# Late u, k and q tiles of the in projection by a wide and a narrow pass; low parts of every third half by an adding transfer

## The chip, the cores and the metric

The kernel runs on one core of one Trainium2 chip. The metric is the device time of one execution in microseconds (us), as a median of several runs; less is better. TensorE multiplies, VectorE and ScalarE compute on tiles, GpSimd and SyncE here only issue transfers.

## The reference

One decoder block on x of 256 x 2048 in float32. One input projection feeds two groups; their outputs are joined, projected, added to x and normalised; a gated FFN with a short convolution follows.

```python
# in projection: x (256 x 2048) @ w_in, columns split into
#   u 1024 | q 1024 | k 256 | v 256 | q_idx 1024 | k_idx 64 | w_idx 16
# group A: S5 state-space channels on u (64 groups, 64 states), gelu, GLU
# group B: for each query the index scores q_idx . k_idx (relu, weighted by w_idx)
#          choose the 64 best keys; attention of q on k, v over these, with ALiBi
# x = layer_norm(alpha * x + concat(A, B) @ w_out)
# x = layer_norm(alpha * x + conv_ffn(x))          # d_ff = 5632
def _conv_ffn(x, w_up, w_gate, conv_w, conv_b, w_down):
    h = x @ w_up
    hp = jnp.pad(h, ((0, 0), (CONV_WIDTH - 1, 0), (0, 0)))
    hc = conv_b + sum(conv_w[i] * hp[:, i:i + seq] for i in range(CONV_WIDTH))
    return (jax.nn.gelu(hc, approximate=False) * (x @ w_gate)) @ w_down
```

## The kernel before

**Precision.** Every float32 operand of a large product is held as two parts that TensorE reads: a high part, which a ScalarE copy rounds, and a low part, what is left, which VectorE subtracts. A product is three matmuls into one accumulator: `mm3` (L184 to L188) multiplies high by high (L186), low weights by high x (L187), and high weights by low x (L188). In the in projection each has 128 x 128 weights and 256 columns, the 256 positions.

**Weights.** They stream from HBM in halves of 128 x 1024 float32, 512 KB; the two halves of kw have 640 columns. `load` (L119) issues a half's transfer on SyncE's queue into one of three buffers named raw. `fetch` (L127) makes its parts: ScalarE copies raw into wh (L133), VectorE subtracts into wl (L136). wh and wl have four buffers each. `next_half` (L143) keeps four halves ready ahead of the one in use, and what `fetch` records has high priority. `BY_DMA` (L35) is a set of half numbers; it is empty, so the branch at L137 to L140 is not taken.

**Numbers of the halves.** 0 to 7 the first four u tiles (first halves, then second halves), 8 to 15 the late u tiles 4 to 7, 16 to 31 the eight tiles of qi (the index queries), 32 and 33 kw (index keys and weights), 34 to 37 the two k tiles, 38 to 41 v, 42 to 57 the eight q tiles; then GLU, out projection and FFN.

**Tiles.** `ws_tile` (L288) computes one tile of 128 output columns by 256 positions: 16 k tiles of `mm3` from two halves, 48 matmuls, into an accumulator named acc of which there are two. After each k tile `pump` advances the background jobs by a step: `ssm` (the state-space group: its bu matmuls, VectorE work of 128 x 1024 in `ssm_in`, cbd and dd matmuls in `ssm_out`, tables of sines and gelu on ScalarE) and `indexer` (index scores). One ScalarE copy then takes the tile out of PSUM: into qi, kv or q (L303), or into u (L315), where positions are written in even and odd halves. u is moved on by 64 small transfers for the state-space group. v takes x as the weights and both accumulators at once (L683 to L691).

**The FFN's form.** Up and gate tiles use `wide_half` (L194 to L205): x's high and low part lie side by side, so one matmul of 512 columns multiplies high weights by both, and one of 256 columns multiplies low weights by high x. Eight and eight make a half, 32 matmuls a tile. The two results lie in two parts of the accumulator; a ScalarE copy (L1046) and a VectorE add (L1047) join them.

**What sets the order.** A scheduler orders each engine's instructions by its own estimates and the priorities that the code gives; each engine then works in order. ScalarE's sines and gelus stand in a fixed sequence (`in_turn`), since they load different tables.

Of the kernel before, what the change touches and what calls it, by code (L numbers as in the profile page):

```python
# [11 lines left out]
F32R = mybir.dt.float32r  # L12
I32 = mybir.dt.int32
AF = mybir.ActivationFunctionType
ALU = mybir.AluOpType
# [3 lines left out]
P = 128  # L19
S = 256  # L20
# [11 lines left out]
LEAD = 5  # L32
LAG = 5
PACE = 4
BY_DMA = range(0)  # L35


PRM = {}
# [44 lines left out]
def block_kernel(ctx: ExitStack, tc: tile.TileContext, x_t, x_n, prm_d, cst_d, ssm_d, w_in_d, w_kw_d, w_v_d,  # L83
                 w_glu_d, w_out_d, w_up_d, w_gate4_d, w_gate_d, w_down_d, ln_d, out_d):
    nc = tc.nc
    V, A, G, T = nc.vector, nc.scalar, nc.gpsimd, nc.tensor

    def pool(name, bufs=1, **kw):
        return tc.tile_pool(name=name, bufs=bufs, **kw)
# [5 lines left out]
    ahl = ctx.enter_context(pool("ahl"))  # L95
# [23 lines left out]
    def load():  # L119
# [3 lines left out]
        n = state["next"]  # L123
        raws.append((raw, src.shape[1], special.get(n), src if n in BY_DMA else None))
        state["next"] += 1
# [17 lines left out]
    def next_half():  # L143
        while len(ready) < state["ahead"] and state["next"] < len(halves):
            fetch()
        return ready.pop(0)
# [41 lines left out]
        return T.matmul(out, lhsT=lh[0], rhs=rh[1], start=False, stop=stop).ins  # L188

    def act_tiles(what):  # L190
        return [(t[:, :, 0, :], t[:, :, 1, :])
                for t in (ahl.tile([P, 4, 2, S], F32R, name=f"{what}{j}", tag=f"hl{j}") for j in range(4))]

    def wide_half(out, half, tiles, kh):  # L194


        def passes(low):
            for k in range(8):
                r = tiles[(kh * 8 + k) // 4][:, k % 4]
                yield low, half[low][:, k * P:(k + 1) * P], r[:, 0] if low else r  # L200

        steps = list(passes(1)) + list(passes(0)) if kh else list(passes(0)) + list(passes(1))
        for i, (low, w, r) in enumerate(steps):
            ins = T.matmul(out[:, 0] if low else out, lhsT=w, rhs=r, start=kh == 0 and i == 0, stop=kh == 1 and i == 15)  # L204
        return ins.ins  # L205

    def kt_of(tiles, kt):
        h, l = tiles[kt // 4]
        return h[:, kt % 4, :], l[:, kt % 4, :]
# [6 lines left out]
    tmp = ExitStack()  # L216
    at = ctx.enter_context(pool("att", side="right"))
    st = tmp.enter_context(pool("ssmt", side="right"))
    xt = act_tiles("x")
    raw_b = st.tile([P, 2, 512], F32, name="raw_b", tag="t3")  # L220
    raw_c = proj.tile([P, 2, 512], F32, name="raw_c", tag="kv")

# [49 lines left out]
    def acc_tile():  # L272
        return ps.tile([P, 512], F32, name="acc", bufs=2)
# [14 lines left out]
    def ws_tile(evac, m=P):  # L288

        acc = acc_tile()  # L290
        for kt in range(16):
            if kt % 8 == 0:
                half = next_half()
            c = (kt % 8) * m
            mm3(acc[:m, :S], (half[0][:, c:c + m], half[1][:, c:c + m]), kt_of(xt, kt), kt == 0, kt == 15)
            pump()
        with tc.high_priority():
            evac(acc)

    def proj_tile(name, t=None):  # L300
        if t is None:
            t = proj.tile([P, S], F32, name=name)
        ws_tile(lambda acc: A.activation(t, acc[:, :S], AF.Copy))  # L303
        return t

    def proj_four(name):
        t = proj.tile([P, 4, S], F32, name=name)
        return [proj_tile(name, t[:, i]) for i in range(4)]


    ut, yt, hs = [], [], {}

    def u_tile(ct, acc):
        t = proj.tile([P, 2, P], F32, name=f"u{ct}")
        A.activation(t.rearrange("p two k -> p k two"), acc[:, :S].rearrange("p (k two) -> p k two", two=2), AF.Copy)  # L315
        ut.append(t)

    bu = psb.tile([P, 2, 2, 512], F32, name="bu")
# [1 line left out]
    for kh in range(2):  # L320
        for ct in range(4):
            half = next_half()
# [91 lines left out]
    two, p = exp_parts(pc("ldt"))  # L414
# [19 lines left out]
    two, p = exp_parts(tt(dt, a_re, ALU.mult))  # L434
# [59 lines left out]
    for ct in range(8):  # L494
        tp = misc_tile()
        for h in range(2):
            for ri in range(2):
                k = (h * 2 + ri) * P
# [119 lines left out]
    for ct in range(4, 8):  # L618
        if ct == SSM_FROM:
            add_bg(ssm_job, 1)  # L620
        ws_tile(lambda acc: u_tile(ct, acc))


    qit = proj_four("qi0") + proj_four("qi1")
    kw = proj.tile([P, S], F32, name="kw")[0:80]
    ws_tile(lambda acc: A.activation(kw, acc[:80, :S], AF.Copy), m=80)
    ki2 = proj.tile([P, S], F32, name="ki2")
# [52 lines left out]
    for kt in range(16):  # L680
        if kt % 4 == 0:
            half = next_half()
# [75 lines left out]
    mix = [None, None, (post.tile([P, 4, S], F32R, name="mixh"), post.tile([P, 4, S], F32R, name="mixl")), None]  # L758
# [9 lines left out]
    drain()  # L768


    hl_tiles = [ahl.tile([P, 4, 2, S], F32R, name=f"mix{j}", tag=f"hl{j}") for j in range(4)]
    hl = [(t[:, :, 0, :], t[:, :, 1, :]) for t in hl_tiles]
    mix = [hl[0], hl[1], mix[2], hl[3]]
    def glu_products(acc, half, kts):
        for kt in kts:
# [11 lines left out]
    for nt in range(8):  # L787
        h, l = mix[nt // 4]
        if nt < 2:
            acc = first_glu[nt][0]  # L790
        else:
            acc = glu_acc(nt)
# [127 lines left out]
    def row_banks(i):  # L920
# [6 lines left out]
    beside = {2: a01.scores, 3: a01.weights, 6: a00.turn, 7: a10.turn, 9: a00.values, 10: a10.values,  # L927
              11: a11.scores, 12: a11.weights, 14: a01.turn, 17: a01.values, 22: a11.turn, 25: a11.values}
    unit = 0
    with tc.manual_schedule(engines={mybir.EngineType.PE}):  # L930
        for some in (range(4), range(4, 6), range(6, 8)):
# [6 lines left out]
            for db in range(3):  # L938
                for i in some:
                    half = next_half()  # L940
# [97 lines left out]
    with pool("pd", space=PSUM) as pd:  # L1038
        for f in range(NF):
            pu = []  # L1040
            for which in range(1 if f < 4 else 2):
                p = pd.tile([P, 2, S], F32, name=f"pd{which}", bufs=2)
                for kh in range(2):
                    last = wide_half(p, next_half(), h1t, kh)
                t = ff.tile([P, S], F32, name=f"sum{which}", bufs=2)
                A.activation(t, p[:, 1], AF.Copy)  # L1046
                V.tensor_tensor(t, t, p[:, 0], op=ALU.add)  # L1047
                pu.append(t)
            if f < 4:

                if f % 2 == 0:
                    gt = pe0.tile([P, 2, S], F32, name="gt", tag=f"e0{f // 2}")
                with tc.issue_after(last):
                  for b in range(2):
                    T.transpose(gt[:, f % 2, b * 128:(b + 1) * 128], gate4[b][:, f * 128:(f + 1) * 128], ident)
            up, gate = pu if f >= 4 else (pu[0], gt[:, f % 2])
            hc = ff.tile([P, S], F32, name="hc", bufs=2)
            A.activation(hc, up, AF.Identity, scale=pc("cw2", f), bias=pc("cb", f))
            V.scalar_tensor_tensor(hc[:, 1:], up[:, :S - 1], pc("cw1", f), hc[:, 1:], op0=ALU.mult, op1=ALU.add)
            V.scalar_tensor_tensor(hc[:, 2:], up[:, :S - 2], pc("cw0", f), hc[:, 2:], op0=ALU.mult, op1=ALU.add)  # L1060
            in_turn(hc, hc, AF.Gelu)
            done = V.tensor_tensor(act[:, f, :], hc, gate, op=ALU.mult).ins
            if f == 4:
                load_ln(0)
            if f == 16:
                load_ln(1)
            if 8 <= f < 14:

                b, db = (f - 8) // 3, (f - 8) % 3 + 1
                cs = slice(db * 512, (db + 1) * 512)  # L1070
                zs = z[:, b, cs]
                with tc.issue_after(done):
                    V.tensor_tensor(zs, zs, ln_t["g"][:, cs], op=ALU.mult)
                    V.tensor_tensor(zs, zs, ln_t["b"][:, cs], op=ALU.add)
# [107 lines left out]
    for f in range(NF):  # L1182
        if f == NF - 8 * LAG:
            state["ahead"] = 2 * LAG
        hl = act_split(f)
        for d2 in range(2):
            half = next_half()
# [103 lines left out]
```

## Time and profile before

| | us |
|---|---|
| median of three runs | 1108.07 |
| the three runs | 1108.05, 1111.54, 1108.07 |
| the profiled execution | 1109.74 |
| its span in the trace | 1108.0 |
| TensorE busy | 1092.8 (99%) |
| VectorE busy | 740.2 (67%) |
| ScalarE busy | 579.2 (52%) |
| GpSimd busy | 0.2 |

The span is from the first to the last instruction of the trace; the execution's own time has 1.7 us more around it. PE is TensorE, DVE VectorE, ACT ScalarE, POOL GpSimd, SP SyncE. Busy times of matmuls overlap, since each begins before the one ahead of it has ended; the pace is read from their starts. L133 is line 133 of the kernel.

### The profile page before, as it was taken

How to read it: one execution, taken by the hardware profiler on the slowest of the kernel's cores; microseconds unless marked ns; L12 is line 12 of the kernel's file. 1: busy time of each engine (PE TensorE's matmuls, PEld its weight loads, DVE VectorE, ACT ScalarE, POOL GpSimd, SP SyncE). 2: the span in 40 equal slices, each digit the busy share in tenths (PEclk: the TensorE clock that was granted, in tenths of full speed). 3: DMA queues.
4: the chain of work that ended last, by engine and by line, in shares of the span. 5: the costliest groups of instructions: out<-in, count | busy, mean ns of one | idle time of the engine just before them, and what ended most of it. 6: DMA issues, size and time to landing. Idle time of an engine off the chain costs nothing.

```text
span 1108.0 us, 16918 instructions
## 1 busy us (share of the span) xinstructions
PE 1092.8 (99%) x6599; PEld 948.2 (86%) x6599; DVE 740.2 (67%) x1054; ACT 579.2 (52%) x878; POOL 0.2 (0%) x4
## 2 busy tenths in 40 slices
PE   8999999999999999999999999999999999999997
PEld 7899998899778888888888888888888888888885
DVE  6969889687558666677666656565656556565547
ACT  5965664457544765555454545454545445454430
POOL 0000000000000000000000000000000000000000
PEclk9999999999999999999999999999999999999999
DMA  7644434246466455555665555555555566665522
GB/s 254 231 147 136 129 132 170 97 140 241 159 225 206 164 198 191 190 189 190 253 204 190 190 191 189 189 192 190 187 190 189 186 227 220 211 225 198 198 101 76
DMA packets 59311, 204.44 MB, mean 185 GB/s; under 512 B 7264, under 2 KB 10080, under 8 KB 58592
## 3 DMA queue, kind: packets, MB, share of 16 engines
q1 hardware_dynamic: 59232, 203.38, 54.0%
q8 instruction: 51, 0.84, 0.3%
q14 instruction: 28, 0.23, 0.1%
HBM read 200.20 MB, written 2.10 MB: 183 GB/s over the span
## 4 chain that ended last, share of the span: by engine, by line
PE 86%; DVE 7%; ACT 2%; DMA 2%; issue 2%; SPq 1%; ACTq 0%; DVEq 0%
PE pd L204 42%; PE e L188 7%; PE e L187 7%; PE e L186 7%; PE acc L187 3%; PE acc L188 3%; PE acc L186 3%; PE o L186 3%; PE o L188 3%; PE o L187 3%; DVE wl L136 2%; PE misc L650 1%; DMA raw<-in_w_in_dram 1%; ACT wh L133 1%; PE glu L187 1%
## 5 line engine op out<-in xcount | busy, mean ns | idle before, releaser
L136 DVE TENSOR_TENSOR wl<-raw,wh 128x1024 fp32r<-128x1024 f32 x299 | 364.8, 1222 | 251.4 <-ACT wh L133 248.2
L133 ACT ACTIVATE wh<-raw 128x1024 fp32r<-128x1024 f32 x299 | 315.3, 1056 | 251.8 <-PE pd L204 135.7
L204 PE MATMUL pd<-mix,wh 128*128 128x512 f32 x1344 | 321.4, 391 | 0.7 <-ACT gate L1018 0.7
L204 PEld LDWEIGHTS pd<-mix,wh 128*128 128x128 f32 x1344 | 246.7, 188 | 48.8 <-ACT gate L1018 1.1
L204 PEld LDWEIGHTS pd<-mix,wl 128*128 128x128 f32 x1344 | 172.4, 191 | 6.6
L204 PE MATMUL pd<-mix,wl 128*128 128x256 f32 x1344 | 174.8, 283 | 0.0
L186 PE MATMUL acc<-x,wh 128*128 128x256 f32 (+1 forms) x400 | 114.5, 288 | 3.7 <-ACT wh L133 1.8
L187 PE MATMUL acc<-x,wl 128*128 128x256 f32 (+1 forms) x400 | 115.2, 288 | 0.5 <-DVE wl L182 0.3
L188 PE MATMUL acc<-x,wh 128*128 128x256 f32 (+1 forms) x400 | 114.8, 288 | 0.8 <-DVE x L182 0.8
L136 DVE TENSOR_TENSOR wxl<-raw,wxh 128x1024 fp32r<-128x1024 f32 x42 | 51.5, 1225 | 45.8 <-ACT wxh L133 44.1
L186 PEld LDWEIGHTS acc<-x,wh 128*128 128x128 f32 (+1 forms) x400 | 76.3, 191 | 5.8 <-ACT wh L133 2.0
L188 PEld LDWEIGHTS acc<-x,wh 128*128 128x128 f32 (+1 forms) x400 | 76.6, 191 | 3.2 <-issue 1.6
L187 PEld LDWEIGHTS acc<-x,wl 128*128 128x128 f32 (+1 forms) x400 | 76.5, 191 | 3.1 <-issue 1.2
L133 ACT ACTIVATE wxh<-raw 128x1024 fp32r<-128x1024 f32 x42 | 44.6, 1061 | 57.8 <-DMA raw<-in_w_down_dram 25.8
L187 PE MATMUL e<-wh,acthl 128*128 128x512 f32 (+1 forms) x154 | 59.5, 386 | 0.0
L186 PE MATMUL e<-wh,acthl 128*128 128x512 f32 (+1 forms) x154 | 59.4, 387 | 0.0
L188 PE MATMUL e<-wl,acthl 128*128 128x512 f32 (+1 forms) x154 | 58.7, 386 | 0.0
L175 ACT ACTIVATE hc<-hc 128x256 f32<-128x256 f32 x44 | 18.4, 417 | 76.2 <-DVE hc L1060 76.2
L186 PE MATMUL e<-wxh,acthl 128*128 128x512 f32 (+1 forms) x130 | 50.1, 386 | 0.0
L187 PE MATMUL e<-wxh,acthl 128*128 128x512 f32 (+1 forms) x130 | 50.1, 386 | 0.0
L188 PE MATMUL e<-wxl,acthl 128*128 128x512 f32 (+1 forms) x130 | 50.1, 386 | 0.0
L1047 DVE TENSOR_TENSOR sum<-sum,pd 128x256 f32<-128x256 f32 x84 | 34.7, 413 | 0.0
(299 smaller groups left out, 1455.5 us busy)
## 6 DMA issues: line engine op xcount, KB each, us to landing
raw<-in_w_gate_dram SPq DMA_DIRECT2D x88, 512.0 KB, 4.0
raw<-in_w_up_dram SPq DMA_DIRECT2D x88, 512.0 KB, 3.9
raw<-in_w_down_dram SPq DMA_DIRECT2D x88, 512.0 KB, 4.5
raw<-in_w_in_dram SPq DMA_DIRECT2D x51, 512.0 KB, 4.3
raw<-in_w_out_dram SPq DMA_DIRECT2D x32, 512.0 KB, 4.0
raw<-in_w_glu_dram SPq DMA_DIRECT2D x8, 512.0 KB, 3.6
raw<-in_w_v_dram SPq DMA_DIRECT2D x4, 512.0 KB, 3.8
z<-in_x_n_dram SPq DMA_DIRECT2D x1, 2048.0 KB, 10.5
```

The costliest lines, as they stand in the source:

```text
L133: A.activation(h[:, :w], raw[:, :w], AF.Copy)
L136: V.tensor_sub(l[:, :w], raw[:, :w], h[:, :w].bitcast(F32))
L175: ins = A.activation(*args, **kw)
L186: T.matmul(out, lhsT=lh[0], rhs=rh[0], start=start, stop=False)
L187: T.matmul(out, lhsT=lh[1], rhs=rh[0], start=False, stop=False)
L188: return T.matmul(out, lhsT=lh[0], rhs=rh[1], start=False, stop=stop).ins
L204: ins = T.matmul(out[:, 0] if low else out, lhsT=w, rhs=r, start=kh == 0 and i == 0, stop=kh == 1 and i == 15)
L650: T.matmul(banks[e][:, (hp % 2) * w:(hp % 2 + 1) * w], lhsT=qit[hp][r, b * 128:(b + 1) * 128], rhs=ki2[r, 0:w], start=True, stop=True)
L1047: V.tensor_tensor(t, t, p[:, 0], op=ALU.add)
```

## The change

Late u (tiles 4 to 7), the two k tiles and the eight q tiles, 14 tiles, are computed by `wide_tile`: two calls of `wide_half`, with `pump` after each of the 16 narrow matmuls. In a tile's first half the eight wide matmuls come first, in its second half the eight narrow ones. The first four u tiles, qi, kw and v keep `mm3`. A wide tile's two results are joined by `add_parts`, a ScalarE copy and a VectorE add; the FFN uses the same function for the same work as before. u's tiles are now read from PSUM in even and odd halves and written in one piece.

`BY_DMA` holds 13 halves: 20, 23, 26, 29 (qi), 32 (kw), 35 (second half of the first k tile), 38, 41 (v), 44, 47, 50, 53, 56 (q). In these the branch in `fetch` is taken: ScalarE writes raw, negated and rounded like the high part, into wl (L139), and a transfer on GpSimd's queue reads the half from HBM a second time and adds it to wl there (L140), which leaves the low part. VectorE's subtract (L136) is left out for them.

```diff
@@ -32,7 +32,7 @@
 LEAD = 5
 LAG = 5
 PACE = 4
-BY_DMA = range(0)
+BY_DMA = range(20, 58, 3)
 
 
 PRM = {}
@@ -188,10 +188,12 @@
         return T.matmul(out, lhsT=lh[0], rhs=rh[1], start=False, stop=stop).ins
 
     def act_tiles(what):
-        return [(t[:, :, 0, :], t[:, :, 1, :])
-                for t in (ahl.tile([P, 4, 2, S], F32R, name=f"{what}{j}", tag=f"hl{j}") for j in range(4))]
-
-    def wide_half(out, half, tiles, kh):
+        return [ahl.tile([P, 4, 2, S], F32R, name=f"{what}{j}", tag=f"hl{j}") for j in range(4)]
+
+    def both_parts(tiles):
+        return [(t[:, :, 0, :], t[:, :, 1, :]) for t in tiles]
+
+    def wide_half(out, half, tiles, kh, beside=lambda: None):
 
 
         def passes(low):
@@ -202,7 +204,13 @@
         steps = list(passes(1)) + list(passes(0)) if kh else list(passes(0)) + list(passes(1))
         for i, (low, w, r) in enumerate(steps):
             ins = T.matmul(out[:, 0] if low else out, lhsT=w, rhs=r, start=kh == 0 and i == 0, stop=kh == 1 and i == 15)
+            if low:
+                beside()
         return ins.ins
+
+    def add_parts(t, hi, lo):
+        A.activation(t, lo, AF.Copy)
+        V.tensor_tensor(t, t, hi, op=ALU.add)
 
     def kt_of(tiles, kt):
         h, l = tiles[kt // 4]
@@ -216,7 +224,8 @@
     tmp = ExitStack()
     at = ctx.enter_context(pool("att", side="right"))
     st = tmp.enter_context(pool("ssmt", side="right"))
-    xt = act_tiles("x")
+    x_tiles = act_tiles("x")
+    xt = both_parts(x_tiles)
     raw_b = st.tile([P, 2, 512], F32, name="raw_b", tag="t3")
     raw_c = proj.tile([P, 2, 512], F32, name="raw_c", tag="kv")
 
@@ -297,22 +306,37 @@
         with tc.high_priority():
             evac(acc)
 
-    def proj_tile(name, t=None):
+    def wide_tile(evac):
+
+        acc = acc_tile().rearrange("p (two s) -> p two s", two=2)
+        for kh in range(2):
+            wide_half(acc, next_half(), x_tiles, kh, pump)
+        with tc.high_priority():
+            evac(acc[:, 0], acc[:, 1])
+
+    def proj_tile(name, t=None, wide=True):
         if t is None:
             t = proj.tile([P, S], F32, name=name)
-        ws_tile(lambda acc: A.activation(t, acc[:, :S], AF.Copy))
+        if wide:
+            wide_tile(lambda hi, lo: add_parts(t, hi, lo))
+        else:
+            ws_tile(lambda acc: A.activation(t, acc[:, :S], AF.Copy))
         return t
 
-    def proj_four(name):
+    def proj_four(name, wide=True):
         t = proj.tile([P, 4, S], F32, name=name)
-        return [proj_tile(name, t[:, i]) for i in range(4)]
+        return [proj_tile(name, t[:, i], wide) for i in range(4)]
 
 
     ut, yt, hs = [], [], {}
 
-    def u_tile(ct, acc):
+    def u_tile(ct, acc, lo=None):
         t = proj.tile([P, 2, P], F32, name=f"u{ct}")
-        A.activation(t.rearrange("p two k -> p k two"), acc[:, :S].rearrange("p (k two) -> p k two", two=2), AF.Copy)
+        acc, lo = (a if a is None else a[:, :S].rearrange("p (k two) -> p two k", two=2) for a in (acc, lo))
+        if lo is None:
+            A.activation(t, acc, AF.Copy)
+        else:
+            add_parts(t, acc, lo)
         ut.append(t)
 
     bu = psb.tile([P, 2, 2, 512], F32, name="bu")
@@ -618,10 +642,10 @@
     for ct in range(4, 8):
         if ct == SSM_FROM:
             add_bg(ssm_job, 1)
-        ws_tile(lambda acc: u_tile(ct, acc))
-
-
-    qit = proj_four("qi0") + proj_four("qi1")
+        wide_tile(lambda hi, lo: u_tile(ct, hi, lo))
+
+
+    qit = proj_four("qi0", False) + proj_four("qi1", False)
     kw = proj.tile([P, S], F32, name="kw")[0:80]
     ws_tile(lambda acc: A.activation(kw, acc[:80, :S], AF.Copy), m=80)
     ki2 = proj.tile([P, S], F32, name="ki2")
@@ -768,8 +792,8 @@
     drain()
 
 
-    hl_tiles = [ahl.tile([P, 4, 2, S], F32R, name=f"mix{j}", tag=f"hl{j}") for j in range(4)]
-    hl = [(t[:, :, 0, :], t[:, :, 1, :]) for t in hl_tiles]
+    hl_tiles = act_tiles("mix")
+    hl = both_parts(hl_tiles)
     mix = [hl[0], hl[1], mix[2], hl[3]]
     def glu_products(acc, half, kts):
         for kt in kts:
@@ -1043,8 +1067,7 @@
                 for kh in range(2):
                     last = wide_half(p, next_half(), h1t, kh)
                 t = ff.tile([P, S], F32, name=f"sum{which}", bufs=2)
-                A.activation(t, p[:, 1], AF.Copy)
-                V.tensor_tensor(t, t, p[:, 0], op=ALU.add)
+                add_parts(t, p[:, 0], p[:, 1])
                 pu.append(t)
             if f < 4:
```

Three places of the order. First TensorE at the start of u tile 4, before; x_81 to x_84 are the four tiles of x, bu holds two of the first four u tiles' sums:

```order
L188 MATMUL bu<-x_84,wh 128x256
L186 MATMUL acc<-x_81,wh 128x256
L187 MATMUL acc<-x_81,wl 128x256
L188 MATMUL acc<-x_81,wh 128x256
L186 MATMUL acc<-x_81,wh 128x256
```

And after:

```order
L188 MATMUL bu<-x_84,wh 128x256
L206 MATMUL acc<-x_81,wh 128x512 x4
L206 MATMUL acc<-x_82,wh 128x512 x4
L206 MATMUL acc<-x_81,wl 128x256 x4
L206 MATMUL acc<-x_82,wl 128x256 x4
L186 MATMUL bu<-x_83,wh 128x256
```

Where the triple of three passes went on k tile by k tile, four wide matmuls on each of two tiles of x now stand, then four narrow ones on each.

Second ScalarE at the second k tile. Its evacuation is the ACTIVATE into kv; cs, y and dd belong to the state-space group, the table load to its gelus, ki to the index keys. Before:

```order
L303 ACTIVATE kv<-acc 128x256
L133 ACTIVATE wh<-raw 128x1024 x2
L353 ACTIVATE cs<-cst,f_420 128x128 x8
L303 ACTIVATE kv<-acc 128x256
L133 ACTIVATE wh<-raw 128x1024
L175 ACTIVATE cs<-cs 128x1024
L585 ACTIVATE dd<-cst,prm 128x128
L361 ACTIVATE cs<-cs 128x1024
L599 ACTIVATE y_1651<-misc 128x2x128
L599 ACTIVATE y_1653<-misc 128x2x128
L175 ACTIVATE cs<-cs,cst 128x1024
L175 ACT_TABLE_LOAD
```

And after:

```order
L175 ACT_TABLE_LOAD
L175 ACTIVATE y_1055<-y_1055 128x256
L175 ACTIVATE y_1057<-y_1057 128x256
L175 ACTIVATE y_1322<-y_1322 128x256
L175 ACTIVATE y_1324<-y_1324 128x256
L175 ACTIVATE y_1594<-y_1594 128x256
L175 ACTIVATE y_1596<-y_1596 128x256
L133 ACTIVATE wh<-raw 128x1024
L609 ACTIVATE dd<-cst,prm 128x128
L659 ACTIVATE ki_1899<-misc 128x256
L139 ACTIVATE wl<-raw 128x1024
L212 ACTIVATE kv<-acc 128x256
```

Before, both evacuations into kv stood ahead of the run from the cs copy to the gelus of y; now the second stands behind the run and behind the copies after it, the negated one of L139 among them.

Third GpSimd's queue after; before, it had no transfer:

```order
L140 DMA wl<-in_w_in_dram 128x1024 x4
L140 DMA wl<-in_w_kw_dram 128x640
L140 DMA wl<-in_w_in_dram 128x1024
L140 DMA wl<-in_w_v_dram 128x1024 x2
L140 DMA wl<-in_w_in_dram 128x1024 x5
```

Thirteen adding transfers moved in there, and nothing else is on that queue.

## Rows read from the trace of the kernel before

**Rows 1.** page: busy us, share, count by engine; the chain's shares

```profile
PE 1092.8 (99%) x6599; PEld 948.2 (86%) x6599; DVE 740.2 (67%) x1054; ACT 579.2 (52%) x878; POOL 0.2 (0%) x4
...
PE 86%; DVE 7%; ACT 2%; DMA 2%; issue 2%; SPq 1%; ACTq 0%; DVEq 0%
```

**Rows 2.** by stage: us, busy PE PEld DVE ACT POOL, PEclk, DMA share, GB/s

```profile
80.00:100.00 20.00, 19.98 (x183) 18.13 (x185) 20.00 (x17) 13.17 (x23) 0.00 (x0) 1.00 0.40 123
100.00:120.00 20.00, 20.00 (x206) 18.90 (x199) 20.00 (x17) 10.23 (x25) 0.00 (x0) 1.00 0.37 121
165.00:175.00 10.00, 8.94 (x54) 8.00 (x53) 10.00 (x10) 5.99 (x14) 0.00 (x0) 0.83 0.38 128
500.00:600.00 100.00, 100.00 (x576) 88.39 (x576) 64.50 (x87) 51.07 (x72) 0.00 (x0) 1.00 0.60 210
```

**Rows 3.** TensorE's timeline, 88 us: start, length, line, [idle before, releaser]

```profile
88.63 0.28 PE L186 MATMUL acc<-x,wh 128*128 128x256 f32 x1
...
91.51 0.28 PE L186 MATMUL acc<-x,wh 128*128 128x256 f32 x1
```

**Rows 4.** TensorE's timeline in the FFN, 498 to 508 us

```profile
498.89 3.82 PE L204 MATMUL pd<-mix,wh 128*128 128x512 f32 x16
502.55 2.08 PE L204 MATMUL pd<-mix,wl 128*128 128x256 f32 x16
504.46 3.82 PE L204 MATMUL pd<-mix,wh 128*128 128x512 f32 x16
```

**Rows 5.** TensorE's timeline, start of the late u tiles

```profile
35.90 0.38 PE L186 MATMUL acc<-x,wh 128*128 128x256 f32 x1 [1.75 <-ACT wh L133]
```

**Rows 6.** TensorE's timeline, 169 to 171 us

```profile
169.12 0.65 PE L186 MATMUL acc<-x,wh 128*128 128x256 f32 x2 [0.85 <-ACT kv L691]
...
170.89 0.41 PE L186 MATMUL acc<-x,wh 128*128 128x256 f32 x1
171.10 0.41 PE L187 MATMUL acc<-x,wl 128*128 128x256 f32 x1
```

**Rows 7.** chain that ended last, 70 to 172 us: start, length, what

```profile
151.88 2.27 DVE wl L136 x2
```

**Rows 8.** ScalarE's timeline, 147 to 166 us

```profile
147.29 0.36 ACT L303 ACTIVATE kv<-acc 128x256 f32<-128x256 f32 x1
...
154.27 0.36 ACT L303 ACTIVATE kv<-acc 128x256 f32<-128x256 f32 x1
...
158.25 1.06 ACT L175 ACTIVATE cs<-cs 128x1024 f32<-128x1024 f32 x1 [2.67 <-DVE cs L359]
...
162.14 1.28 ACT L175 ACT_TABLE_LOAD   x1
...
164.99 1.05 ACT L133 ACTIVATE wh<-raw 128x1024 fp32r<-128x1024 f32 x1
```

**Rows 9.** tile sum (FFN): duration ns min/median/max, first to last start us, shapes

```profile
L1046 ACT ACTIVATE sum<-pd x84: 362/363/367, 395.1 to 858.3; 128x256 f32<-128x256 f32 x84
L1047 DVE TENSOR_TENSOR sum<-sum,pd x84: 412/413/423, 396.4 to 860.3; 128x256 f32<-128x256 f32 x84
```

**Rows 10.** tile u, the same view

```profile
L315 ACT ACTIVATE u<-acc x6: 621/628/645, 27.7 to 62.6; 128x256 f32<-128x256 f32 x6
```

**Rows 11.** tile raw, the same view, 60 to 240 us

```profile
L136 DVE TENSOR_TENSOR wl<-raw,wh x45: 824/1224/1236, 59.4 to 239.0; 128x1024 fp32r<-128x1024 f32 x43, 128x640 fp32r<-128x640 f32 x2
L133 ACT ACTIVATE wh<-raw x44: 738/1051/1090, 60.7 to 237.9; 128x1024 fp32r<-128x1024 f32 x42, 128x640 fp32r<-128x640 f32 x2
```

**Rows 12.** DMA issues, 60:240, then whole run: KB, us to landing

```profile
raw<-in_w_in_dram SPq DMA_DIRECT2D x32, 512.0 KB, 3.9
...
xraw<-in_x_t_dram SPq DMA_DIRECT2D x3, 512.0 KB, 6.5
```

**Rows 13.** line 303 on ScalarE, the same view, 60 to 260 us

```profile
L303 ACT ACTIVATE qi<-acc x8: 362/364/385, 74.1 to 131.3; 128x256 f32<-128x256 f32 x8
L303 ACT ACTIVATE q<-acc x8: 384/384/395, 178.6 to 237.6; 128x256 f32<-128x256 f32 x8
```

## The prediction

> **What bounds the kernel now.** I read the page's busy shares, clock and chain first. TensorE is busy 99% of the span, and 86% of the chain lies on it [rows 1]: an edit pays if it shortens TensorE's own work, or one of the few places where TensorE waits. VectorE at 67% and ScalarE at 52% are means. The table by stage shows VectorE busy all of its 20 us in both stretches of the in projection, with TensorE full beside it (19.98 and 20.00), while in the FFN VectorE is at 64.50 of 100 [rows 2]. So in the in projection VectorE runs as full as TensorE; its busy rows overlap, so 20.00 of 20 doesn't say how much it could still take.
>
> Then the pace of the matmuls. The same line comes at 88.63 and, eight k steps of three passes later, at 91.51 [rows 3]: 24 matmuls in 2.88 us, 0.12 us each, and a tile of two halves is 5.76 us. In the FFN sixteen 512-column matmuls go from 498.89 to 502.55, 3.66 us, and sixteen 256-column ones from 502.55 to 504.46, 1.91 us [rows 4]: a tile of the same depth is 5.57 us.
>
> Then the waits. TensorE's list shows two between 30 and 240 us. (a) At the start of the late u tiles the first matmul comes at 35.90 after 1.75 us of waiting for a ScalarE copy of weights [rows 5]. (b) At 169.12 it waits 0.85 us for a copy on ScalarE; by 170.89 matmuls of 256 columns start 0.21 apart (170.89, 171.10), the half clock of 1.2 GHz [rows 6]. The stretch from 165 to 175 us has TensorE busy 8.94 of 10 at a granted clock of 0.83 [rows 2], so (b) costs 1.06 us of idling and (1 - 0.83) x 10 = 1.7 us of slow clock, 2.75 in all. The chain shows where (b) comes from: two low parts back to back on VectorE at 151.88, in the middle of a chain of VectorE work [rows 7], and then ScalarE's run of table work, from the cs copy at 158.25 over the table load at 162.14 to the next weight copy at 164.99, 6.7 us, behind the evacuation of k at 154.27 [rows 8].
>
> **The change part by part. Passes.** 14 tiles go from 48 matmuls of 256 columns to 16 of 512 and 16 of 256, the FFN's own form. 5.76 - 5.57 = 0.19 us a tile, 2.66 us for 14. Of tile u4 the first half stands behind (a), so I take 2.6. All of it is on the path, since TensorE hardly waits there.
>
> First the row: a 512-column matmul takes 3.66/16 = 0.229 us, 0.011 less than two of 256 [rows 3, 4]. The Trainium skill, "TensorE: Matmul & The Clock Gate", section "Back-to-back issue gap", gives an isolated gap of N/2.4 + 2.5 ns, by which one pair merged saves 2.5 ns; an estimate from that page is 224 x 2.5 ns = 0.56 us for the change. The trace's FFN rows disagree with that size, and I go by them.
>
> **Evacuation.** A wide tile ends with a ScalarE copy (0.363 us) and a VectorE add (0.413), where before one copy did [rows 9]. That is 14 x 0.41 = 5.8 us more on VectorE and nothing more on ScalarE. The accumulator has two buffers, so it is free again for the tile after next, a whole tile of 5.57 us later; the 84 FFN evacuations of this form show no waiting TensorE at that distance, and a VectorE instruction of 1.1 to 2.3 us ahead of the add fits as well. If that cover were gone, an add late by one 1.13 us instruction in each of 14 tiles would cost up to 16 us, but nothing in the order takes the cover away. u's copies wrote with a stride (0.628 us [rows 10]) and now read PSUM with one: nothing shows that price, so it lies between 0.363 and 0.628, a gain of at most 0.27 for each of the two in stall (a). I take nothing.
>
> **Low parts.** 13 halves (every third from 20 to 56; one is of kw, 640 columns) lose their VectorE subtract. These start 1.13 us apart when back to back (2.27 for two [rows 7]), the short one takes 0.82 [rows 11]: 12 x 1.13 + 0.82 = 14.4 us off VectorE. With the adds VectorE is relieved by 14.4 - 5.8 = 8.6 us. ScalarE gets 13 copies of the negated weights: 12 x 1.05 + 0.74 = 13.3 us [rows 11]; it is busy 10 to 13 of 20 us there [rows 2], so its share rises to about 0.6 or 0.7 and the sum is hidden. The place can matter: such a copy waits for its low buffer, which frees when TensorE has done the half four before, and behind it on ScalarE's queue stand the next weight copies, the SSM's scaled copies and the evacuations. The copy to the high buffer before it waits for the same half already, so the wait is not longer, only the work behind it by 1.05 us.
>
> **Adding transfers.** 13 transfers of 512 KB on GpSimd's queue, where there were none. That queue holds nothing else, so nothing is queued behind a waiting one but the next; SP keeps its loads. The trace has no adding transfer. Plain loads land in 3.9 us: the lower bound. Three sharing the engines took 6.5 [rows 12], and twice 3.9 (if the target is read as well) is 7.8: the upper bound. I take about 6, near the 6.5 row, since these meet SP's loads in flight. The cover: the low buffer comes round after four halves, so three halves of TensorE lie between its release and its use. Evacuations of qi span 74.1 to 131.3 for eight tiles, 8.17 us a tile with the background work, q 178.6 to 237.6, 8.43 [rows 13], and the two of k are 154.27 - 147.29 = 6.98 apart [rows 8]: three halves are 12.3, 12.6 and 10.5 us, and never under 3 x 2.88 = 8.6. Less the copy's 1.05 a transfer may take 11 us in qi and q, 9.4 at k and v, 7.6 with no background at all. Both bounds fit but for the last case, 0.2 us over. Cost: nothing.
>
> The Trainium skill, "DMA: Bandwidth & Descriptors", section "Anatomy of one DMA — SWDGE (gpsimd) path", gives 2.0 us plus bytes/436e3 us for this queue, an estimate of 3.2 us here. This kernel's plain loads took 3.9, above it; by the page no transfer could be late either.
>
> **ScalarE's run.** The rebuilt order puts the run [rows 8] ahead of the second k tile's evacuation; before, that copy (154.27) stood ahead of it. v takes over one accumulator and the index work a third of the copies behind it, so TensorE may wait there for the end of the run. I bound it by nothing (the run is over in time, VectorE's relief having pulled it forward) and the 6.7 us of the run less one tile's cover of which TensorE has at least a half, 2.88: 3.8, plus 1.7 of half clock. Stall (b), which this would replace, gives 2.75 back. So -2.75 to +2.75 against the forecast, up to 5 if the run itself starts later. I take nothing, the middle.
>
> **Sum.** Profiled execution: 1109.74 us, span 1108.0 and 1.7 around it. 1109.74 - 2.6 = 1107.1. The median of the three runs, 1108.07, is 1.67 lower; carried over, **1105.5**.
>
> **The rivals.**
>
> B, VectorE's relief also clears stall (b). For: the chain into (b) runs on VectorE, and 8.6 us of its work go. Against: the run on ScalarE stays, and 13.3 us are added there. 1105.5 - 2.75 = 1102.7.
>
> C, the k evacuation behind ScalarE's run costs more than (b) did: 1105.5 plus 1 to 5, middle 1108.5. For: the order. Against: two accumulators, and the run may come earlier.
>
> D, the other side: adding transfers land late. TensorE then waits for the low part of a half, with the half clock behind each wait. It decides at 9.4 us from issue to landing at kw, k and v (four transfers). At 10 us these are late by 0.6 (10.5 cover) to 2.4 (bare 8.6): 4 x (0.6 + 1.7) = 9.2, 4 x (2.4 + 1.7) = 16.4; time 1114.7 to 1121.9, and about 1113 if not each stall drops the clock. For: no row shows an adding transfer. Against: it would have to take over 2.4 times a plain load.
>
> E, the wide pass saves nothing, the time going by columns alone: 3 x 256 = 512 + 256. 1108.1. By the page named above it would be 1107.5. Against: 0.229 against 2 x 0.12 [rows 3, 4].
>
> **How the numbers follow.** A measurement of this kernel tells 0.3%, 3.3 us, from no change: faster is under 1104.75, slower over 1111.4. The forecast (waits unchanged in sum) gets 0.42, of which 0.10 below 1104.75, as its 2.6 us are just short of the bound; B 0.28; C 0.12, of which 0.03 over 1111.4; D 0.13; E 0.05. Faster 0.10 + 0.28 = 0.38; same 0.32 + 0.09 + 0.05 = 0.46; slower 0.03 + 0.13 = 0.16. The range goes from 1101.5 (B, with 0.54 us of u's copies and some clock) to 1113, the lower edge of D, and leaves out most of D and a tail of B. The forecast's own range is 1104 to 1107.5.
>
> **What would show it.** Passes: in the late u, k and q tiles sixteen wide matmuls in 3.66 us. Low parts: 14.4 us fewer of subtracts between 60 and 240, VectorE idle there by some 8 us. Transfers: issue to landing under 9 us, and no TensorE wait whose releaser is a transfer into wl. B or C: the stretch around 170 us without the 0.83 clock, or with a longer wait for a kv copy. I am wrong if a new wait of TensorE is put down to those transfers, or to ScalarE at another place of qi and q, where its copies have pushed an evacuation or a weight copy out.

## The result, and the profile after

The changed kernel takes 1116.23 us, the median of 13 runs (1111.12 to 1121.21), against 1109.56 of before in 13 runs beside it (1107.72 to 1111.54): ratio 1.0061, 95% interval 1.0049 to 1.0072. It is 6.7 us slower; the forecast was 1105.5 and the range ended at 1113. The runs of the changed kernel spread with the granted clock: 1111.12 us at a mean of 0.997, 1121.21 at 0.988, and 0.009 of 1116 us is the 10 us between them. The profiled execution took 1115.43 us, its span is 1113.4, 5.4 more than that of before.

TensorE's busy time is the same to 0.1 us, so the passes' gain has gone into something else; the line of the page after, as in [rows 1]:

```profile
PE 1092.7 (98%) x6375; PEld 937.8 (84%) x6375; DVE 731.8 (66%) x1055; ACT 590.4 (53%) x891; POOL 11.6 (1%) x17
```

The list of what TensorE waited for between 20 and 250 us in the kernel after (us in all, times, longest):

```profile
PE bu L575 <- DMA ustk<-u: 3.4, 1, 3.4
PE acc L206 <- DVE u L213: 1.7, 1, 1.7
PE misc L674 <- ACT rel L680: 1.4, 1, 1.4
PE bu L186 <- ACT u L337: 1.2, 1, 1.2
PE acc L187 <- DMA wl<-in_w_kw_dram: 0.2, 1, 0.2
```

The longest is not for a low part but for ustk, one of the small transfers that hand u tiles to the state-space group; a low part by an adding transfer is waited for once, for 0.2 us. TensorE's timeline of the kernel after, around the longest wait:

```profile
80.03 2.08 PE L575 MATMUL bu<-ustk,bt 64*128 64x128 f32 x12 [3.44 <-DMA ustk<-u]
...
83.06 0.41 PE L186 MATMUL acc<-x,wh 128*128 128x256 f32 x1
83.27 0.41 PE L187 MATMUL acc<-x,wl 128*128 128x256 f32 x1
...
92.83 0.28 PE L187 MATMUL acc<-x,wl 128*128 128x256 f32 x1
92.94 0.28 PE L188 MATMUL acc<-x,wh 128*128 128x256 f32 x1
```

Behind it matmuls start 0.21 apart, the half clock of 1.2 GHz; at 92.83 again 0.11 to 0.12. The table by stage of the kernel after, columns as in [rows 2]:

```profile
0.00:20.00 20.00, 15.97 (x80) 11.68 (x81) 13.13 (x42) 9.74 (x11) 0.20 (x4) 0.91 0.82 270
78.00:93.00 15.00, 12.97 (x58) 11.50 (x59) 12.55 (x12) 5.80 (x16) 0.00 (x0) 0.54 0.14 42
165.00:175.00 10.00, 10.00 (x81) 9.49 (x79) 10.00 (x9) 5.17 (x10) 0.86 (x1) 1.00 0.62 159
```

and the same stretch of the kernel before:

```profile
78.00:93.00 15.00, 14.98 (x121) 14.02 (x124) 15.00 (x13) 11.63 (x25) 0.00 (x0) 1.00 0.34 103
```

A granted clock of 0.54 over 15 us takes 6.9 us, about 0.8 of which falls into the wait itself: the place costs 3.44 + 6.1 = 9.5 us. The stretch of stall (b), 165 to 175 us, is full and at clock 1.00, where [rows 2] had 8.94 and 0.83. With the two other new waits, 1.67 and 1.43 us, a half clock in the first 20 us (0.09 x 20 = 1.8; it comes in some of the profiles below and not in others), less the passes' 2.6, stall (b)'s 2.75 and 2.9 at (a), the sum is +6.2; the spans say +5.4, so 0.8 us are not placed. Place (a) cost more before than the prediction counted: from 30 to 37 us TensorE was idle for 2.32 us, and from 37 to 41 the granted clock was 0.57, which is 1.7 more; after, it is idle there for 1.19 us at a clock of 1.00.

Where the late u transfer comes from is read in the chain of waits, and in GpSimd's timeline, of the kernel after:

```profile
72.09 7.90 DMA ustk<-u
```

```profile
70.81 1.01 POOL L140 DMA_DIRECT2D wl<-in_w_in_dram  x1 [70.36 <-ACT wl L139]
```

The first adding transfer, half 20's, is issued at 70.81; a u transfer of 16 KB issued at 72.09 lands 7.90 us later. The DMA view between 72 and 80 us, for the kernel before (KB each, us to landing):

```profile
ustk<-u SPq DMA_DIRECT2D x11, 16.0 KB, 1.8
```

and for the kernel after, with the queues ahead of it (packets, MB, share of 16 engines; q0 is GpSimd's):

```profile
q0 software_dynamic: 144, 0.52, 46.2%
q1 hardware_dynamic: 528, 0.66, 24.3%
...
raw<-in_w_in_dram SPq DMA_DIRECT2D x1, 512.0 KB, 8.3
ustk<-u SPq DMA_DIRECT2D x8, 16.0 KB, 6.3
```

The u transfers go from 1.8 to 6.3 us, and the weight load among them takes 8.3 instead of 4.0. That load is the link between the two. SyncE's queue in the kernel after:

```profile
71.52 0.52 SPq L122 DMA_DIRECT2D raw<-in_w_in_dram  x1
72.09 8.89 SPq L554 DMA_DIRECT2D ustk<-u  x9
```

The load is issued ahead of these u transfers, on their own queue. It lands at 71.52 + 8.3 = 79.8, and the u transfer issued next at 72.09 + 7.90 = 79.99. In the kernel before it is the same on a smaller scale: a load issued at 75.81 lands after 4.0 us, at 79.8, and the u transfer behind it, issued at 76.38, at 80.0:

```profile
ustk<-u SPq DMA_DIRECT2D x1, 16.0 KB, 3.6
```

So the 1.8 us of the kernel before belong to u transfers without a load ahead of them. The adding transfer lengthens the load, and the u transfers behind the load come in after it. From the page of the kernel after, the whole run:

```profile
wl<-in_w_in_dram POOLq DMA_DIRECT2D x10, 512.0 KB, 8.3
```

### The profile page after: what moved, and what is told of

Same layout as the page of the kernel before. It is cut to its first block, busy times and chain, and to the rows that moved or that the text cites. A ratio compares the mean times of both kernels' runs of the same rounds, so it can differ in the third digit from the quotient of the medians.

```text
span 1113.4 us, 16514 instructions
## 1 busy us (share of the span) xinstructions
PE 1092.7 (98%) x6375; PEld 937.8 (84%) x6375; DVE 731.8 (66%) x1055; ACT 590.4 (53%) x891; POOL 11.6 (1%) x17
## 4 chain that ended last, share of the span: by engine, by line
PE 88%; issue 4%; DMA 4%; DVE 3%; ACT 1%; POOL 0%; SPq 0%; POOLq 0%; ACTq 0%; DVEq 0%
PE pd L206 42%; PE e L188 7%; PE e L186 7%; PE e L187 7%; PE acc L206 6%; PE o L186 3%; PE o L188 3%; PE o L187 3%; DMA raw<-in_w_in_dram 2%; PE acc L187 1%; PE acc L186 1%; PE acc L188 1%; PE misc L674 1%; DMA wl<-in_w_kw_dram 1%; DMA ustk<-u 1%
## 5 line engine op out<-in xcount | busy, mean ns | idle before, releaser
L136 DVE TENSOR_TENSOR wl<-raw,wh 128x1024 fp32r<-128x1024 f32 x286 | 349.4, 1223 | 260.9 <-ACT wh L133 255.6
L136 DVE TENSOR_TENSOR wxl<-raw,wxh 128x1024 fp32r<-128x1024 f32 x42 | 51.5, 1226 | 42.1 <-ACT wxh L133 40.2
L206 PE MATMUL acc<-x,wh 128*128 128x512 f32 x224 | 56.6, 396 | 1.8 <-DVE u L213 1.7
L186 PE MATMUL acc<-x,wh 128*128 128x256 f32 (+1 forms) x176 | 52.2, 297 | 1.8 <-ACT x L181 1.8
L187 PE MATMUL acc<-x,wl 128*128 128x256 f32 (+1 forms) x176 | 52.7, 300 | 0.2 <-DMA wl<-in_w_kw_dram 0.2
L188 PE MATMUL acc<-x,wh 128*128 128x256 f32 (+1 forms) x176 | 52.0, 295 | 0.8 <-DVE x L182 0.8
L206 PEld LDWEIGHTS acc<-x,wh 128*128 128x128 f32 x224 | 40.3, 188 | 10.9 <-DVE u L213 2.1
L186 PEld LDWEIGHTS acc<-x,wh 128*128 128x128 f32 (+1 forms) x176 | 34.9, 198 | 2.8 <-ACT x L181 2.0
L187 PEld LDWEIGHTS acc<-x,wl 128*128 128x128 f32 (+1 forms) x176 | 34.9, 199 | 1.3 <-issue 0.6
```

The source lines that it names most:

```text
L136: V.tensor_sub(l[:, :w], raw[:, :w], h[:, :w].bitcast(F32))
L186: T.matmul(out, lhsT=lh[0], rhs=rh[0], start=start, stop=False)
L187: T.matmul(out, lhsT=lh[1], rhs=rh[0], start=False, stop=False)
```

## The experiments

Theory T: the bytes of half 20's adding transfer hold up the u transfers; TensorE waits, then runs at half clock. Rivals: W, the wide tiles cost; O, the new order does it; M, each of the 13 transfers costs its share. Times are medians, with the kernel before run beside them; ratios are to that. Edits are against the changed kernel where nothing else is said.

**e1, no adding transfers.**

```diff
-BY_DMA = range(20, 58, 3)
+BY_DMA = range(0)
```

> The change without its adding transfers: the wide tiles alone, all low parts by VectorE's subtract. Theory T: the loss comes from the first adding transfer (half 20), which holds up the small u transfers of the second state-space batch; TensorE waited 3.44 us for one at 80 us and then ran 13.65 us at half clock, about 10 us together. Then this kernel has no such wait and shows the passes' gain of 2.6 us: 1107 us against 1109.6 of before. Theory W: the wide tiles themselves cost (the VectorE add of a u tile, behind which TensorE waited 1.67 us at 49.82, and the moved background steps): no faster than before, 1109.5 to 1112.

1107.05 us against 1108.56, ratio 0.9980 (0.9970 to 0.9991), 2.2 us faster. Its list of TensorE's waits, 20 to 250 us:

```profile
PE acc L206 <- DVE u L213: 1.9, 1, 1.9
PE bu L575 <- DMA ustk<-u: 1.4, 1, 1.4
```

T's time is met: the wide tiles alone win about the 2.6 us that their passes are worth. That the two numbers agree is partly luck, since the 2.2 are a net of the passes, of old stalls that are gone and of new waits. W has a part too: the wait for the add of a u tile is there without any adding transfer, and so is a short wait for u. Stall (b) is gone as well, with all subtracts still on VectorE:

```profile
165.00:175.00 10.00, 10.00 (x73) 9.15 (x73) 10.00 (x10) 5.83 (x12) 0.00 (x0) 1.00 0.33 107
```

**e2, adding transfers on three-pass tiles.**

```diff
-    def proj_tile(name, t=None, wide=True):
+    def proj_tile(name, t=None, wide=False):
...
-    def proj_four(name, wide=True):
+    def proj_four(name, wide=False):
...
-        wide_tile(lambda hi, lo: u_tile(ct, hi, lo))
+        ws_tile(lambda acc: u_tile(ct, acc))
```

> The adding transfers alone: all tiles of the in projection by three passes, as before, and the same 13 halves by an adding transfer. T: the long wait for a u transfer near 80 us comes back with the half clock behind it, 1109.6 plus about 7 to 10 = 1117 to 1120. W: no loss, 1107 to 1110.

1122.22 us, ratio 1.0116 (1.0097 to 1.0135): 13 us slower. TensorE's timeline and table by stage:

```profile
78.21 1.86 PE L575 MATMUL bu<-ustk,bt 64*128 64x128 f32 x8 [2.32 <-DMA ustk<-u]
...
191.35 0.39 PE L187 MATMUL acc<-x,wl 128*128 128x256 f32 x1 [1.80 <-DMA wl<-in_w_in_dram]
```

```profile
78.00:93.00 15.00, 14.79 (x59) 13.00 (x60) 12.73 (x12) 5.40 (x14) 0.00 (x0) 0.50 0.14 42
```

The wait for u comes back without wide tiles, and with it the half clock (0.50 here, and 0.84 from 93 to 110 us: 0.50 x 15 + 0.16 x 17 = 10.2 us). Beside it low parts come late, three waits of 2.8 us in all, which is the prediction's rival D. The time lies 2.2 us above T's span.

**e3, half 20 alone left out.**

```diff
-BY_DMA = range(20, 58, 3)
+BY_DMA = range(23, 58, 3)
```

> The change without half 20's adding transfer alone: 12 of the 13 stay. T: the wait near 80 us is gone, the later transfers fall among fewer u transfers and are hidden: 1106 to 1108. Rival M: each of the 13 costs about half a microsecond by slowing the plain loads (5.3 us to landing instead of 4.3): 1115 to 1116.

1108.47 us, ratio 0.9997 (0.9986 to 1.0008). One transfer of 13 carried the loss here: against the change this is 7 us. Against e1, though, the other 12 give nothing and take some 1.9 us (0.9997 - 0.9980 of 1109; the two intervals overlap a little). The order of the engines changes with it, so e5 was made.

**e5, half 20's transfer thinned, order kept.**

```diff
-        raws.append((raw, src.shape[1], special.get(n), src if n in BY_DMA else None))
+        raws.append((raw, src.shape[1], special.get(n), (src, n) if n in BY_DMA else None))
...
-                G.dma_start(out=l[:, :w], in_=src, accum_op=ALU.add)
+                G.dma_start(out=l[:, :8 if src[1] == 20 else w], in_=src[0][:, :8 if src[1] == 20 else w], accum_op=ALU.add)
```

(`load` now hands on the half's number beside the source: `src[1]` and `src[0]`. Half 20's low part is complete in 8 columns only.)

> The change with half 20's adding transfer cut from 1024 to 8 columns, so that this half's low part is left wrong; the order of every engine's instructions is the changed kernel's own. It takes away the bytes of that transfer and nothing else. T (its bytes in the transfer engines hold up the u transfers): no wait for u near 80 us, full clock from 78 to 92 us, 1106 to 1108. Theory O (the new order: SyncE issues a weight load between the u transfers, three of them earlier): the wait stays above 2 us, 1113 to 1117.

1108.44 us, ratio 0.9994 (0.9982 to 1.0007). Its DMA view from 72 to 80 us and its table by stage:

```profile
q0 software_dynamic: 144, 0.00, 2.8%
...
ustk<-u SPq DMA_DIRECT2D x11, 16.0 KB, 1.8
```

```profile
78.00:93.00 15.00, 14.12 (x232) 12.68 (x223) 15.00 (x14) 11.02 (x27) 0.87 (x1) 1.00 0.22 56
```

Every engine works in the order of the changed kernel; only bytes are gone. The load among the u transfers lands in 3.6 us instead of 8.3, the u transfer behind it in 3.2 instead of 7.9; their median is back at 1.8, the clock at 1.00, and 7.4 us of the ratio are back. The new order by itself (O) falls, and T is shown: the bytes of half 20's transfer cost this time. The new order still has a part in the way it comes about, as it puts five u transfers ahead of the load where there were nine; no run takes the load from there and leaves the adding transfer.

**e7, half 20's transfer plain.**

```diff
-                G.dma_start(out=l[:, :w], in_=src, accum_op=ALU.add)
+                G.dma_start(out=l[:, :w], in_=src[0], accum_op=ALU.bypass if src[1] == 20 else ALU.add)
```

(With the other line of e5. Half 20's low part is overwritten here by the half itself.)

> The change with half 20's transfer made a plain one: same queue, same 512 KB from HBM, same place and order on every engine, but wl is overwritten instead of added to, so that half's low part is wrong. A (the adding makes the transfer long, since it also reads what it writes to): it lands in 4 to 6 us instead of 8.6, the u transfers beside it in 2.5 to 4.5, TensorE's wait near 80 us falls below 1.5 us: 1108 to 1110. B (any second transfer of 512 KB at that place does it): the wait stays above 2.5 us with the long half clock behind it: 1113 to 1117.

1111.29 us, ratio 1.0010 (0.9988 to 1.0032), with ten runs from 1105.65 to 1116.79. DMA view from 72 to 80 us:

```profile
q0 software_dynamic: 144, 0.52, 28.6%
...
wl<-in_w_in_dram POOLq DMA_DIRECT2D x1, 512.0 KB, 5.8
...
ustk<-u SPq DMA_DIRECT2D x10, 16.0 KB, 4.0
```

The time is between A and B, nearer to A, and TensorE's wait for u is 1.4 us, as in A. The same bytes without the adding take 28.6% of the engines instead of 46.2%, land in 5.8 us, and hold the u transfers at 4.0. The u transfer that SyncE issued right behind this transfer, with no load ahead of it, took

```profile
ustk<-u SPq DMA_DIRECT2D x1, 16.0 KB, 4.8
```

so a large transfer of another queue can hold up a u transfer directly as well; in the changed kernel the one in that place took 2.0, and those that came late stood behind the load. By the landings the second transfer does a part and the adding the rest. By the times only the adding's part is clear, 0.0051 of the ratio; the plain transfer's 0.0016 against e5 is within the intervals. The run of 1105.65 had a mean granted clock of 0.997 and that of 1116.79 one of 0.991, so this kernel seems to be at the edge of the long half clock.

**e6, all 13 thinned.**

```diff
-                G.dma_start(out=l[:, :w], in_=src, accum_op=ALU.add)
+                G.dma_start(out=l[:, :8], in_=src[0][:, :8], accum_op=ALU.add)
```

(With the other line of e5. The 13 low parts are complete in 8 columns only.)

> The change with all 13 adding transfers cut to 8 columns, so that the low parts of these halves are left wrong; the copies on ScalarE stay and the subtracts on VectorE stay away. Against the kernel that thins half 20 alone (1108.44 us) it takes away the bytes of the other 12. T2: these cost little: TensorE waited 1.4 us for wl in that kernel's profile, so 1106.5 to 1107.5. Rival M: the 12 slow every load (7.0 us to landing instead of 4.1) and the time with it: below 1105.

1107.58 us, ratio 0.9980 (0.9965 to 0.9995), the ratio of e1. So with the bytes gone, taking 13 subtracts off VectorE and putting 13 copies on ScalarE is worth nothing that can be measured. Against e5 the bytes of the other 12 transfers cost about 1.6 us, which is within the two intervals; and from about 165 us on VectorE and ScalarE work in another order here than in the changed kernel, so that the bytes aren't the only difference.

**e13, three-pass tiles, half 20 left out (edit of e2, and that of e3).**

> Adding transfers alone on three-pass tiles (1122.2 us with all 13), without half 20's. T (that first transfer carries the loss through the u transfers, whatever the passes): 1110 to 1114, with about 3 us of waits for wl left. M (each transfer costs its share): 1120 to 1121.

1116.02 us, ratio 1.0075 (1.0059 to 1.0091). Half 20 is worth 4.5 us here, but 8.3 us of loss stay. TensorE's timeline and table by stage:

```profile
183.24 0.38 PE L187 MATMUL acc<-x,wl 128*128 128x256 f32 x1 [3.12 <-DMA wl<-in_w_in_dram]
...
239.95 0.39 PE L187 MATMUL acc<-x,wl 128*128 128x256 f32 x1 [2.12 <-DMA wl<-in_w_in_dram]
```

```profile
180.00:195.00 15.00, 11.88 (x94) 8.88 (x92) 1.26 (x4) 4.00 (x9) 0.86 (x1) 0.66 0.49 143
```

Neither theory's time is met. Two low parts are late by 5.2 us together, and the first brings a half clock, 0.34 x 15 = 5.1 us: rival D's price, in a kernel other than the changed one. On three-pass tiles a half's first low matmul comes 0.12 us after its first high one; on a wide tile's first half it comes eight wide matmuls, 8 x 0.229 = 1.8 us, later. That this is why the changed kernel was spared is only argued, and it can't be all: a wide tile's second half begins with its narrow matmuls, and two of the five q halves (47 and 53) are second halves.

**e9, 13 wide tiles, no adding transfers (edit of e1 and this).**

```diff
-        wide_tile(lambda hi, lo: u_tile(ct, hi, lo))
+        if ct == 4:
+            ws_tile(lambda acc: u_tile(ct, acc))
+        else:
+            wide_tile(lambda hi, lo: u_tile(ct, hi, lo))
```

> The wide tiles without adding transfers, and u tile 4 by three passes: 13 wide tiles. The first VectorE add of u, behind which TensorE waited 1.9 us at 49 us with a half clock of 3.4 us behind it (1.7 us) in the kernel of 14 wide tiles, is gone, and the next one stands behind VectorE's setup work. If that add is what eats the passes' gain: 1107.05 - 3.6 + 0.2 = 1103.7. Rival: the wait moves to the next tile or to the weights before the late u tiles (1.75 us before the change): 1106.5 to 1108.

1104.55 us against 1109.30, ratio 0.9951 (0.9930 to 0.9973): faster than both kernels. The wait at 50 us did not go, though; it has another releaser:

```profile
50.30 2.11 PE L206 MATMUL acc<-x,wh 128*128 128x512 f32 x8 [2.11 <-ACT u L337]
```

What went is the half clock behind it (granted clock from 40 to 60 us: 1.00, in e1 0.91), and e1's wait for ustk. So the add was not the main cause of the wait. In the kernel after, ScalarE's copy of u4 comes at 48.35, where in the kernel before it came at 46.04; the rebuilt order has setup work (cos, cbd) ahead of it. ScalarE's timeline before, then after, and VectorE's add and TensorE after:

```profile
46.04 0.63 ACT L315 ACTIVATE u<-acc 128x256 f32<-128x256 f32 x1
```

```profile
48.35 0.36 ACT L212 ACTIVATE u<-acc 128x256 f32<-128x256 f32 x1
```

```profile
49.36 0.41 DVE L213 TENSOR_TENSOR u<-u,acc 128x256 f32<-128x256 f32 x1
```

```profile
49.82 2.11 PE L206 MATMUL acc<-x,wh 128*128 128x512 f32 x8 [1.67 <-DVE u L213]
```

The copy starts 2.3 us later, and the add ends 1.4 us behind the copy's start: both together used up the tile of cover.

**e8, k and q alone wide (edit of e1, and `ws_tile` for all late u).**

> Wide passes for k and q alone (10 tiles), all u tiles by three passes, no adding transfers. In the kernel of 13 wide tiles (1104.55 us) TensorE still waited 2.11 us at 50.30 us, now for ScalarE's copy of a u tile, which stands behind setup work, and 1.76 us at 149.57 for a low part with a half clock behind it. If the wide u tiles make the first wait, it goes here, and three tiles give back 0.19 us each: 1104.55 - 2.1 + 0.6 = 1103. Rival: the weights before the late u tiles take the wait back, as before the change (1.75 us and a half clock): 1105 to 1107.

1107.01 us, ratio 0.9978 (0.9967 to 0.9989). The wait at 50 us is gone, as expected, but the time is not below e9's; it lies at the end of the rival's span, but the rival's wait for weights is 1.2 us here, at a granted clock of 1.00. Inconclusive, since every wait left in its list is at most 1.2 us.

**e10, as e9, and the eight qi tiles wide.**

```diff
-    qit = proj_four("qi0", False) + proj_four("qi1", False)
+    qit = proj_four("qi0") + proj_four("qi1")
```

> As the kernel with u tile 4 by three passes, and the eight qi tiles wide too: 21 wide tiles, no adding transfers. By the passes 8 x 0.19 = 1.5 us less than that kernel, 1102 if it is at 1103.7. Rival: in qi VectorE is busy 20 of 20 us, eight adds of 0.41 us come on top and TensorE waits for low parts: 1 to 3 us more than that kernel.

1111.90 us, ratio 1.0019 (1.0004 to 1.0034), 7.5 us over e9. TensorE's longest wait from 225 to 400 us:

```profile
PE o L186 <- ACT sgm L175: 2.9, 1, 2.9
```

The last q tile comes out 2.3 us earlier than in e9 (231.5 against 233.8) and the first FFN tile 5.8 later (396.9 against 391.1): the in projection won its passes, and the out projection then waited for the gate of the state-space group (sgm), which is made 3.6 us later than in e9 (from 244.4 against 240.8). The rival had the sign and the wrong place: not low parts in qi. Of the 5.8 us 2.9 are this wait; the rest is not placed.

**e11 and e12, as e9, with adding transfers behind the u transfers.**

```diff
-BY_DMA = range(0)
+BY_DMA = range(35, 58, 3)
```

e12 has (34, 38) instead.

> The kernel of 13 wide tiles (u tile 4 by three passes, 1104.55 us) with adding transfers for every third half from 35 on: k, v and q, eight of them, after nearly all u transfers. Theory R: there the transfers do what they are for; VectorE is relieved of about 9 us and the wait of 1.76 us for a low part at 149.57 with the half clock behind it goes: 1101 to 1102.5. Theory L: at 7 to 9 us to landing they come late at k and v and slow the loads: TensorE waits 1 to 3 us for wl or raw: 1105 to 1109.

> The same kernel of 13 wide tiles with two adding transfers only, halves 34 and 38, on either side of the wait for a low part at 149.57 us. R: the wait shrinks by the 1.13 us of one subtract and the half clock may go with it: 1102 to 1103.5. L: 1104.5 to 1106.

e11: 1111.42 us, ratio 1.0039 (1.0024 to 1.0054), 9.8 us over e9 by the ratios. e12: 1105.19, ratio 0.9969 (0.9957 to 0.9981), the same as e9 within the intervals. In e11 TensorE waits in the list from 20 to 400 us for:

```profile
PE acc L186 <- ACT wh L133: 2.5, 2, 1.6
PE acc L188 <- DMA wl<-in_w_v_dram: 2.3, 1, 2.3
```

L has the mechanism right: away from the u transfers the adding transfers land late themselves, and the weight copies with them; e11's time is 2.4 us above L's span. R's times fail in both. In e12 the wait for a low part near 149.57 us, 1.8 us in e9, is gone, and the time is no lower: relieving VectorE bought nothing that can be measured.

## Why the prediction was wrong, point by point

**The step that failed** is the adding transfers' "Cost: nothing". It asked whether wl would be there for its own reader, and in the changed kernel it was, but for 0.2 us. It let SP's loads in flight lengthen the adding transfer, and did not ask what the adding transfer does to them and to what stands behind them in SyncE's queue. The row for that was in the trace of before, the 64 u transfers of 16 KB in 2.6 us (whole run):

```profile
ustk<-u SPq DMA_DIRECT2D x64, 16.0 KB, 2.6
```

and TensorE's background matmuls read them. In the place of "nothing" stand 7.4 us for half 20 alone (e5), and 9.0 for all 13 (1.0061 against e1's 0.9980). The way there is a weight load that lands in 8.3 us instead of 4, the u transfers behind it, a wait of 3.44 us and the half clock that follows.

**The bounds of one transfer**, 3.9 to 7.8 us, with 6 taken, were low: 8.3 is the median of ten. The Trainium skill, "DMA: Bandwidth & Descriptors", section "Anatomy of one DMA — SWDGE (gpsimd) path", by which none could be late, gave an estimate of 3.2 us. The runs disagree and the measurement decides: 8.3 with the adding, 5.8 for the plain transfer of e7 beside a weight load.

**The price of a wait**, 1.7 us of half clock behind each, came from stall (b). Behind the wait of 3.44 us it was 6.1.

**"Waits unchanged in sum"**: two old stalls that the forecast left standing went, (b) and most of (a), 5.6 us together. Beside the wait for u, new ones of 1.67 and 1.43 us came.

**The evacuation's cover**, "nothing in the order takes the cover away", failed at u4: 1.67 us. The order printed for ScalarE at k was read there, and not at u.

**Passes**: right. 16 wide matmuls take 3.65 us and 16 narrow ones 1.91 in the q tiles of the kernel after, as in [rows 4]; E falls.

```profile
228.87 3.82 PE L206 MATMUL acc<-x,wh 128*128 128x512 f32 x16
232.52 2.08 PE L206 MATMUL acc<-x,wl 128*128 128x256 f32 x16
234.43 3.82 PE L206 MATMUL acc<-x,wh 128*128 128x512 f32 x16
```

e1, with the wide tiles alone, was 2.2 us faster, with an interval of 1.0 to 3.3; the forecast was 2.6. That is a net, with stalls gone and waits new in it; the size of the passes rests on the rows.

**Low parts**: the size was right. The pages before and after:

```profile
L136 DVE TENSOR_TENSOR wl<-raw,wh 128x1024 fp32r<-128x1024 f32 x299 | 364.8, 1222 | 251.4 <-ACT wh L133 248.2
...
L136 DVE TENSOR_TENSOR wl<-raw,wh 128x1024 fp32r<-128x1024 f32 x286 | 349.4, 1223 | 260.9 <-ACT wh L133 255.6
```

It is 15.4 us less, where 14.4 were expected. The sum put its worth at nothing by itself, and e6 against e1 bears that out.

**B**: stall (b) went, but in e1 too, where VectorE was not relieved; so the relief is not what cleared it. What did is open. **C** did not come: no wait for a kv copy is in the changed kernel's list (e6, e8 and e10 have some, of up to 1.0 us). **D** had the right side, and a chance of 0.13; its mechanism showed in e2, e11 and e13, and hardly in the changed kernel, whose time lies in D's span of 1114.7 to 1121.9 for another reason.

Open: why the half clock lasted 13.7 us here and not 3.4 as behind (b), and 0.8 us of the sum.

## What to carry to other kernels

A transfer that is covered for its own reader can still be paid for by others: here it lengthened a load of another queue, and small transfers stood behind that load. When a change adds bytes, list every transfer in flight at that time, what is queued behind it, and who waits for that. Where an engine is busy but not waited for, taking work off it is worth nothing, and what carries the work instead can cost. A change of two parts is tried part by part: here one part won 2.2 us by itself, and 5.4 with one tile left out (e9's ratio), and the other lost more than that.

## What the runs showed of the hardware

The packets of the adding transfer took 46.2% of the 16 engines over 8 us, where the same 0.52 MB without adding (e7) took 28.6%, 1.6 times as long. From the page of the kernel after, over the run:

```profile
q1 hardware_dynamic: 59232, 203.38, 55.4%
q0 software_dynamic: 1872, 6.62, 3.4%
```

Per MB that is 0.51% against 0.27%, 1.9 times.

A transfer of 16 KB that SyncE issued right behind a load of 512 KB landed 0.2 us after that load, whether the load took 4.0 us (before), 3.6 (e5) or 8.3 (after). Without a load ahead it took 1.8 us, and 4.8 in e7 right behind a plain transfer on GpSimd's queue.

And waits of like length cost unlike amounts of half clock: none behind 2.11 us in e9, 10.2 us behind 2.32 in e2, 0.34 x 15 = 5.1 us behind 3.12 in e13, 6.1 behind 3.44 here.
